# Gate reads in four buffers, differential heads asked for earlier, and two norms left unpinned, in a two-layer encoder kernel

## The chip, the cores and the metric

The kernel runs on one core of a Trainium2 chip. The metric is the device time of one execution in microseconds (us), given as the median of several runs. The engines are named as in the profile: PE is TensorE (matmuls and transposes), DVE is VectorE, ACT is ScalarE, POOL is GpSimd, and SP is the engine from whose queue all DMAs of this kernel are issued.

## The reference

Two layers of a bidirectional encoder over 512 tokens of width 1024, all in float32. Each layer computes one combined projection, three kinds of attention, a gated merge and an MLP:

```python
h = _rmsnorm(x, g_mix_pre[l])
z = h @ w_in[l]
...
o_a = _mla(c_q, c_kv, k_r, positions, ...)      # branch 0, 8 heads
o_b = _dilated(dq, dk, dv, rel_bias)            # branch 1
o_c = _diff(fq, fk, fv, positions, rel_bias, ...)  # branch 2, 4 heads, an RMSNorm for each head
gates = jax.nn.sigmoid(gz).reshape(b, s, N_BRANCH, D_MODEL)
merged = (gates[:, :, 0] * (o_a @ w_branch[l, 0])
          + gates[:, :, 1] * (o_b @ w_branch[l, 1])
          + gates[:, :, 2] * (o_c @ w_branch[l, 2]))
x = x + _rmsnorm(merged @ w_out[l], g_mix_post[l])
f = jnp.square(jax.nn.relu(_rmsnorm(x, g_mlp_pre[l]) @ w_up[l])) @ w_down[l]
x = x + _rmsnorm(f, g_mlp_post[l])
```

## The kernel before

**Products.** Every matrix is split into a high and a low part in float32r (names that end in hi and lo: `whi`, `wlo` for weights, `hhi`, `hlo` for the normed input, `moh`, `mol` for an MLA head's output, `ot` pairs for a branch's input). A product is three matmuls, hi·hi, hi·lo and lo·hi (`mm3`). ACT copies the high part, DVE (or POOL) subtracts it to get the low one.

**Order of the work.** The functions call engines in program order. A scheduling layer may reorder instructions on each engine by program order, buffers that come free and its own estimates. Where `in_order(True)` has been called, the wrapper `InOrder` pins ACT, DVE and SP instructions to program order. All DMAs go out through SP's one queue, in the order in which they stand there, so a DMA that waits for its data holds up those behind it. Each DMA also waits until the one eight places ahead of it has landed.

**The start.** x comes in four chunks of 128 tokens. `start(c)` norms a chunk (`norm_scale`: two squares on ACT, a short chain over DVE and POOL, and a scaling of 128x1024 on DVE, giving `xn`) and turns it (`norm_turn`: transposes `ntp` on PE, copies `hhi` on ACT, subtractions `hlo` on DVE). Chunks 0 and 1 are done first. `head_start` then runs the first half (tokens 0 to 255) of four blocks of the projection (`zq`), with `start(2)` behind the third and `start(3)` behind the fourth, and then the second halves. All of this is pinned. In the same stretch of time run `ld` and `lv`, small instructions of the set-up of the differential heads' lambda. A small table product (`pu`) follows on PE.

**The merge.** It runs over branches in the order 1, 2, 0, and in each over eight blocks of 128 output columns (`dp` = 0 to 3, two blocks each). A block is a gate read `gl` (256 KB from `gated` in DRAM), 12 matmuls `bp` into one of the two PSUM buffers of `mmt`, and a DVE operation that multiplies gate and product into `macc` (branch 1) or adds to it. A third block can't start on PE before the `macc` of the first has read its PSUM buffer. Branch 2's inputs are made here by `diff_norm`, once for each of four heads: two loads into `dn` (the head from `ond`, its norm factors from `rdr`), a multiplication on DVE, and an `ot` pair (copy on ACT, subtraction on DVE).

**What comes just ahead of the merge.** The last MLA head ends with matmuls `mo`, a copy `mot` (ACT), a product `ov` (DVE), the parts `moh` (ACT) and `mol` (DVE), and their two stores, which branch 0 reads back. `mot`, `moh` and `mol` live in the pool `tmp` of four buffers. The gates are computed ahead of it, in tiles `gt` with two buffers, and stored to `gated`. In the kernel before, `gl` shares these two buffers.

Of the kernel before, what the change touches and what calls it, by code (L numbers as in the profile page):

```python
# [9 lines left out]
F32 = mybir.dt.float32  # L10
# [56 lines left out]
class InOrder:  # L67


    def __init__(self, tc, eng):  # L70
        self.tc, self.eng, self.on = tc, eng, False

    def __getattr__(self, name):
        fn = getattr(self.eng, name)

        def call(*args, **kw):
            ins = fn(*args, **kw)  # L77
            if self.on:
                self.tc.keep_in_program_order(ins)
            return ins  # L80

        return call


def trunk(tc, a):
    nc = tc.nc
    with ExitStack() as ctx:
        _trunk(ctx, tc, nc, a)


def _trunk(ctx, tc, nc, a):
    sb = ctx.enter_context(tc.tile_pool(name="sb", bufs=1))
    ps = ctx.enter_context(tc.tile_pool(name="ps", bufs=1, space=PSUM))
    dr = ctx.enter_context(tc.tile_pool(name="dr", bufs=1, space=DRAM))
    act, vec, sync = InOrder(tc, nc.scalar), InOrder(tc, nc.vector), InOrder(tc, nc.sync)
    pool, pe = InOrder(tc, nc.gpsimd), nc.tensor

    def in_order(on, engines=(act, vec, sync)):
        for e in engines:
            e.on = on  # L100

    def mmt(name):
        return ps.tile([128, 512], F32, name=name, tag="mm", bufs=2)
# [7 lines left out]
    def pair(name, dt=F32R):  # L111

        t = sb.tile([128, 2, 512], dt, name=name, tag="pair", bufs=13)
        return t[:, 0], t[:, 1]

    def se(name, n, dt=F32):
        return sb.tile([128, n], dt, name=name, tag="se", bufs=6)
# [4 lines left out]
    def tmp(name, dt=F32):  # L122
        return sb.tile([128, 512], dt, name=name, tag="tmp", bufs=4)
# [4 lines left out]
    def f(x):  # L128
        return x.bitcast(F32)
# [4 lines left out]
    def mm3(out, wh, wl, xh, xl, first, last):  # L134
        mul(out, wh, xh, first, False)
        mul(out, wh, xl, False, False)
        mul(out, wl, xh, False, last)
# [50 lines left out]
    def split_w(raw, cols=1024, eng=None):  # L188
        hi = sb.tile([128, 1024], F32R, name="whi", tag="whi", bufs=4)
        lo = sb.tile([128, 1024], F32R, name="wlo", tag="wlo", bufs=4)  # L190
        act.activation(hi[:, :cols], raw[:, :cols], AF.Copy)
        (eng or vec).tensor_tensor(lo[:, :cols], raw[:, :cols], f(hi)[:, :cols], op=OP.subtract)
        return hi, lo

    def weights(src, cols=1024, eng=None):
        return split_w(load_w(src, cols), cols, eng)
# [18 lines left out]
    def norm_scale(x, g):  # L215

        st = small("nst", 2)
        xn = se("xn", D)
        for i in range(2):
            cs = slice(i * 512, (i + 1) * 512)  # L220
            act.activation(xn[:, cs], x[:, cs], AF.Square, accum_out=st[:, i:i + 1])
        vec.tensor_scalar(st[:, 0:1], st[:, 0:1], D * EPS, None, op0=OP.add)
        r = mean_rsqrt("n", st[:, 1:2], st[:, 0:1], D)
        vec.scalar_tensor_tensor(xn, x, r, g, op0=OP.mult, op1=OP.mult)
        return xn
# [156 lines left out]
    def by_chunk(t):  # L382

        return t.rearrange("p (j q) -> p q j", q=4)
# [39 lines left out]
    def chunked(t):  # L424
        return t.rearrange("p (c j) -> p c j", c=4)
# [45 lines left out]
    otd = {}  # L471
# [34 lines left out]
    def layer(l, h, first_w):  # L506
# [283 lines left out]
        for i in range(2):  # L790
            t = sb.tile([128, 512], F32R, name="wk", tag="ql", bufs=3)
# [131 lines left out]
        fill(1000)  # L923


        def diff_norm(hd, out):

            t = se("dn", 1024)
            o, rb = t[:, :512], t[:, 512:]
            sync.dma_start(o, ond[hd])  # L930
            sync.dma_start(rb, bass.AP(tensor=rdr.tensor, offset=rdr.offset + hd * 512, ap=[[0, 128], [1, 512]]))
            vec.tensor_tensor(chunked(o), chunked(o), by_chunk(rb), op=OP.mult)
            act.activation(out[0], o, AF.Copy)
            vec.tensor_tensor(out[1], o, f(out[0]), op=OP.subtract)

        macc = [None] * 8
        mh, ml = [None] * 8, [None] * 8
        for bi, b in enumerate((1, 2, 0)):
            ot = [pair("ot") for _ in range(4)]
            for kc in range(4):  # L940
                if b == 2:
                    diff_norm(kc, ot[kc])
                    continue
                for j in range(2):
                    sync.dma_start(f(ot[kc][j]), otd[b][kc, j])
            for dp in range(4):
                w = weights(wi("w_branch")[b * 4 + dp])
                hi = w[0].rearrange("p (d k n) -> p d k n", d=2, k=4)
                lo = w[1].rearrange("p (d k n) -> p d k n", d=2, k=4)
                for d2 in range(2):  # L950
                    d = dp * 2 + d2
                    t = sb.tile([128, 512], F32, name="gl", tag="gt", bufs=2)
                    sync.dma_start(t, gated[b, d])
                    p = mmt("bp")
                    for k4 in range(4):
                        mm3(p, hi[:, d2, k4], lo[:, d2, k4], ot[k4][0], ot[k4][1], k4 == 0, k4 == 3)
                    if bi == 0:
                        if d2 == 0:
                            mt = sb.tile([128, 2, 512], F32, name="macc", tag="pt", bufs=4)
                        macc[d] = mt[:, d2]  # L960
                        vec.scalar_tensor_tensor(macc[d], t, 1.0, p, op0=OP.add, op1=OP.mult)
                    else:
                        vec.scalar_tensor_tensor(t, t, 1.0, p, op0=OP.add, op1=OP.mult)
                        vec.tensor_tensor(macc[d], macc[d], t, op=OP.add)
                    if bi == 2:
                        mh[d], ml[d] = pair("mrg")
                        act.activation(mh[d], macc[d], AF.Copy, scale=0.5)
                        vec.scalar_tensor_tensor(ml[d], macc[d], 0.5, f(mh[d]), op0=OP.mult, op1=OP.subtract)


        gpost = load_g(wi("g_mix_post"), "gpost")
# [28 lines left out]
        def last_stage(blocks, lhs, xsrc, half_done, done, h_):  # L1000


            xns = {}
            turns = {c: (lambda c=c: norm_turn(xns[c], c, h_)) for c in range(4)}

            def one(acc, w, bi, c):
                hv, lv = (t.rearrange("p (k c) -> p k c", k=2) for t in w)
                for k2 in range(2):
                    k = bi * 2 + k2
                    lh, ll = (t[:, c * 128:(c + 1) * 128] for t in lhs[k])  # L1010
                    mul(acc, lh, hv[:, k2], k == 0, False)
                    mul(acc, lh, lv[:, k2], False, False)
                    mul(acc, ll, hv[:, k2], False, k == 7)

            for c0 in (0, 2):
                xos = {}
                for i in range(2):
                    xos[c0 + i] = se("xo", D)
                    sync.dma_start(xos[c0 + i], xsrc[c0 + i])
                accs = [pst("e0", "t") for _ in range(2)]  # L1020
                for bi in range(4):
                    w = weights(blocks(bi))
                    for i in range(2):
                        one(accs[i], w, bi, c0 + i)
                    if c0 and h_ is not None and bi % 2:
                        turns[bi // 2]()
                for i in range(2):
                    half_done(c0 + i, accs[i])
                accs = [pst("e1", "o") for _ in range(2)]
                ws = [weights(blocks(4 + bi)) for bi in range(4)]  # L1030
                for i in range(2):
                    for bi in range(4):
                        one(accs[i], ws[bi], bi, c0 + i)
                    xns[c0 + i] = done(c0 + i, accs[i], xos[c0 + i])
            return turns
# [5 lines left out]
        def half_out(c, p):  # L1041
# [3 lines left out]
        turns = last_stage(lambda i: wi("w_out")[i], lhs, xin, half_out,  # L1045
                           lambda c, p, xo: finish(ys[c][:, 0], p, ys[c][:, 1], sts[c], xo, c, gpost, xmid, gnext, h2),
                           h2)
# [136 lines left out]
        for qd in range(4):  # L1184
# [32 lines left out]
            last = l == DEPTH - 1  # L1217
# [18 lines left out]
            turns = last_stage(lambda i: wi("w_down")[i], ft, xmid, half_down, down, hn)  # L1236
# [3 lines left out]
    xs, xns, turns = [], {}, {}  # L1240

    def start(c):
        xns[c] = norm_scale(xs[c], g0)
        norm_turn(xns[c], c, h)
# [28 lines left out]
    ws = [split_w(raws[0], eng=pool)]  # L1273
    norm_turn(xns[1], 1, h)
    ws.append(split_w(raws[1]))
    for c in range(2, 4):
        turns[c] = lambda c=c: start(c)
    first = list(head_start(blocks, h, turns, "zq", ws))
    sync.dma_start(flip, a["flip"])
    in_order(False)  # L1280
    setup_bias()
    got = []
    def all_setup():
# [7 lines left out]
    for l in range(DEPTH):  # L1291
        nxt = layer(l, h, first)
        if l + 1 < DEPTH:
            h, turns = nxt
# [91 lines left out]
```

## Time and profile before

| | |
|---|---|
| median of 3 runs | 1870.62 us (1870.53 to 1878.24) |
| the profiled execution | 1869.85 us |
| its span, first to last instruction | 1868.1 us |
| PE busy | 1820.8 us, 97% of the span |
| DVE / ACT / POOL busy | 67% / 51% / 27% |
| mean granted TensorE clock | 0.998 |

The span is what the trace covers; the profiled execution is 1.75 us longer than it, and lies 0.77 us below the median. A granted clock of 1.00 in a stretch means that TensorE ran at the higher of its two levels throughout; 0.50 is the lower. Times of instructions are counted from the start of the span.

### The profile page before, as it was taken

To read this page: it belongs to the slowest core of one execution; us is meant where nothing else is said; L and a number is where in the kernel's file an instruction comes from. 1 tells how busy PE (TensorE), PEld (TensorE's weight loads), DVE (VectorE), ACT (ScalarE), POOL (GpSimd) and SP (SyncE) were. 2 spreads that over 40 slices of the span, in tenths; PEclk is the share of its full clock that TensorE was granted. 3 is DMA by queue.
4 is the path that set the end of the run, shared out by engine and by line. 5 is a ranking of instruction groups with operands and counts; after the bars stand their busy time and mean duration, and the time that the engine had idled before them with its cause. 6 is when DMAs were issued, how large, how long until landed. Compare 5 with 4: busy or idle time off the path is not lost.

```text
span 1868.1 us, 24762 instructions
## 1 busy us (share of the span) xinstructions
PE 1820.8 (97%) x9002; PEld 1523.6 (82%) x9002; DVE 1260.3 (67%) x2024; ACT 960.7 (51%) x1605; POOL 499.1 (27%) x367
## 2 busy tenths in 40 slices
PE   7999999999999999999999999999999999999998
PEld 6788788888777988788888887888887888878886
DVE  4855376656677786888674455675667779587965
ACT  4466355478525453443554554554783354543433
POOL 1344212331000242347123222114200015241542
PEclk9999999999999999999999999999999999999999
DMA  4365554346675432424453333544468562414243
GB/s 161 104 210 195 178 186 136 101 142 194 233 239 204 146 100 81 135 68 149 148 194 107 118 119 119 156 152 121 139 211 276 181 225 68 156 47 152 70 162 136
DMA packets 105843, 281.13 MB, mean 150 GB/s; under 512 B 13470, under 2 KB 19942, under 8 KB 105719
## 3 DMA queue, kind: packets, MB, share of 16 engines
q1 hardware_dynamic: 105718, 279.53, 46.0%
q8 instruction: 71, 1.16, 0.3%
q14 instruction: 54, 0.43, 0.1%
HBM read 228.50 MB, written 39.96 MB: 144 GB/s over the span
## 4 chain that ended last, share of the span: by engine, by line
PE 64%; DVE 10%; issue 4%; POOL 4%; DMA 3%; ACT 2%; SPq 0%; POOLq 0%; DVEq 0%; ACTq 0%
PE up L132 12%; PE gp L132 12%; PE p L132 9%; PE zq L132 7%; PE e L132 5%; PE bp L132 3%; DVE fr L77 3%; DVE wlo L77 3%; PE ms L132 2%; PE tp L465 2%; PE cp L132 2%; PE sd L132 2%; PE mo L132 1%; DVE fs L77 1%; POOL fr L77 1%
## 5 line engine op out<-in xcount | busy, mean ns | idle before, releaser
L77 ACT ACTIVATE whi<-wraw 128x1024 fp32r<-128x1024 f32 (+1 forms) x270 | 283.9, 1054 | 274.6 <-PE up L132 52.8
L77 DVE TENSOR_TENSOR wlo<-wraw,whi 128x1024 fp32r<-128x1024 f32 (+1 forms) x213 | 274.8, 1293 | 142.7 <-ACT whi L77 141.3
L77 POOL TENSOR_TENSOR wlo<-wraw,whi 128x1024 fp32r<-128x1024 f32 x57 | 139.3, 2447 | 369.5 <-ACT whi L77 369.5
L132 PE MATMUL up<-hlo,whi 128*128 128x512 f32 (+1 forms) x576 | 210.4, 366 | 0.0
L132 PE MATMUL up<-hhi,wlo 128*128 128x512 f32 (+1 forms) x576 | 210.4, 366 | 0.0
L132 PE MATMUL up<-hhi,whi 128*128 128x512 f32 (+1 forms) x576 | 209.9, 366 | 0.5 <-ACT hhi L77 0.5
L132 PE MATMUL p<-whi,fs 128*128 128x512 f32 x672 | 208.0, 389 | 0.0
L77 POOL TENSOR_TENSOR dw<-dw 128x1024 f32<-128x1024 f32 x48 | 132.1, 2755 | 144.6 <-DVE wlo L77 143.6
L132 PE MATMUL gp<-hhi,whi 128*128 128x512 f32 x384 | 153.0, 398 | 1.9 <-DVE ql L77 1.9
L132 PE MATMUL gp<-hhi,wlo 128*128 128x512 f32 x384 | 150.8, 393 | 0.3 <-POOL wlo L77 0.3
L132 PE MATMUL gp<-hlo,whi 128*128 128x512 f32 x384 | 150.3, 391 | 0.0
L132 PEld LDWEIGHTS p<-whi,fs 128*128 128x128 f32 x672 | 126.1, 188 | 26.1
L77 DVE TENSOR_TENSOR wlo<-dw,whi 128x1024 fp32r<-128x1024 f32 x84 | 138.0, 1662 | 13.7 <-POOL fr L77 10.9
L132 PE MATMUL zq<-hhi,whi 128*128 128x512 f32 (+1 forms) x384 | 138.7, 364 | 5.5 <-DVE ql L77 2.6
L132 PE MATMUL zq<-hhi,wlo 128*128 128x512 f32 (+1 forms) x384 | 138.7, 362 | 1.7 <-DVE wlo L77 1.0
L132 PE MATMUL zq<-hlo,whi 128*128 128x512 f32 (+1 forms) x384 | 138.3, 361 | 1.7 <-DVE hlo L77 1.7
L132 PE MATMUL p<-wlo,fs 128*128 128x512 f32 x336 | 131.5, 391 | 2.6 <-DVE wlo L77 2.6
L132 PE MATMUL bp<-ot,whi 128*128 128x512 f32 x384 | 120.3, 392 | 4.8 <-DVE macc L77 3.9
L77 ACT ACTIVATE whi<-dw 128x1024 fp32r<-128x1024 f32 x84 | 88.1, 1058 | 68.4 <-PE p L132 42.9
L132 PEld LDWEIGHTS up<-hlo,whi 128*128 128x128 f32 x576 | 108.6, 189 | 17.9 <-DVE hlo L77 0.4
L132 PEld LDWEIGHTS up<-hhi,whi 128*128 128x128 f32 x576 | 108.1, 188 | 18.4 <-ACT hhi L77 1.0
L132 PEld LDWEIGHTS up<-hhi,wlo 128*128 128x128 f32 x576 | 108.6, 189 | 17.5
(257 smaller groups left out, 4053.7 us busy)
## 6 DMA issues: line engine op xcount, KB each, us to landing
wraw<-in_w_up_dram SPq DMA_DIRECT2D x64, 512.0 KB, 4.3
wraw<-in_w_gate_dram SPq DMA_DIRECT2D x48, 512.0 KB, 3.7
dw<-in_w_down_dram SPq DMA_DIRECT2D x48, 512.0 KB, 3.4
btd<-ddram SPq DMA_DIRECT2D x64, 256.0 KB, 3.3
wraw<-in_w_out_dram SPq DMA_DIRECT2D x32, 512.0 KB, 3.4
wraw<-in_w_down_dram SPq DMA_DIRECT2D x32, 512.0 KB, 3.5
wraw<-in_w_dil_dram SPq DMA_DIRECT2D x24, 512.0 KB, 4.7
gated<-gt SPq DMA_DIRECT2D x48, 256.0 KB, 3.0
```

The lines of the kernel that those rows point to most:

```text
L77: ins = fn(*args, **kw)
L132: pe.matmul(out, lhsT, rhs, start=first, stop=last)
L465: pe.transpose(p[:, k * 128:(k + 1) * 128], e[:, k * 128:(k + 1) * 128], perm)
```

## The change

It has three parts.

1. The gate reads `gl` of the merge move from the two buffers that they share with the gate tiles to the pool `tmp` of four buffers, which the last MLA head's `mot`, `moh` and `mol` use too.
2. `diff_norm` becomes a generator. The eight loads of the four heads are called for in branch 1, behind the blocks of `dp` = 1; the arithmetic follows where branch 2 starts.
3. At the start, the pinning ends ahead of `head_start` instead of behind it. The norms of chunks 2 and 3 get a rule of their own: they are issued after the last pinned ACT and the last pinned DVE instruction.

```diff
@@ class InOrder
-        self.tc, self.eng, self.on = tc, eng, False
+        self.tc, self.eng, self.on, self.last = tc, eng, False, None
...
             if self.on:
                 self.tc.keep_in_program_order(ins)
+                self.last = ins.ins
@@ the merge
-        def diff_norm(hd, out):
+        def diff_norm(hd):
...
             sync.dma_start(rb, bass.AP(tensor=rdr.tensor, offset=rdr.offset + hd * 512, ap=[[0, 128], [1, 512]]))
+            yield
+            out = pair("ot")
             vec.tensor_tensor(chunked(o), chunked(o), by_chunk(rb), op=OP.mult)
             act.activation(out[0], o, AF.Copy)
             vec.tensor_tensor(out[1], o, f(out[0]), op=OP.subtract)
+            yield out
...
-            ot = [pair("ot") for _ in range(4)]
-            for kc in range(4):
-                if b == 2:
-                    diff_norm(kc, ot[kc])
-                    continue
-                for j in range(2):
-                    sync.dma_start(f(ot[kc][j]), otd[b][kc, j])
+            if b == 2:
+                ot = [next(n) for n in norms]
+            else:
+                ot = [pair("ot") for _ in range(4)]
+                for kc in range(4):
+                    for j in range(2):
+                        sync.dma_start(f(ot[kc][j]), otd[b][kc, j])
...
-                    t = sb.tile([128, 512], F32, name="gl", tag="gt", bufs=2)
+                    t = tmp("gl")
                     sync.dma_start(t, gated[b, d])
...
+                if b == 1 and dp == 1:
+                    norms = [diff_norm(kc) for kc in range(4)]
+                    for n in norms:
+                        next(n)
@@ the start
+    last = [act.last, vec.last]
+    in_order(False)
+
+    def later(c):
+
+        with tc.issue_after(last[0]), tc.issue_after(last[1]):
+            start(c)
+
     for c in range(2, 4):
-        turns[c] = lambda c=c: start(c)
+        turns[c] = lambda c=c: later(c)
     first = list(head_start(blocks, h, turns, "zq", ws))
     sync.dma_start(flip, a["flip"])
-    in_order(False)
```

How the instructions move, engine by engine, is seen in the order in which they stand. First ACT at the start, as one piece of the difference; `x_93` and `x_97` are chunks 2 and 3, the `whi` that moves is that of the fourth block.

```order
 L77 ACTIVATE whi<-wraw 128x1024 x2
 L77 ACTIVATE xn,nst<-x_93 128x512 x2
+L77 ACTIVATE whi<-wraw 128x1024
+L77 ACTIVATE xn,nst<-x_97 128x512 x2
 L77 ACTIVATE ld<-ld 128x1 x4
-L77 ACTIVATE hhi<-ntp 128x4x128 x2
-L77 ACTIVATE whi<-wraw 128x1024
-L77 ACTIVATE xn,nst<-x_97 128x512 x2
-L77 ACTIVATE hhi<-ntp 128x4x128 x2
+L77 ACTIVATE hhi<-ntp 128x4x128 x4
```

The fourth block's `whi` and the squares of chunk 3 stood behind the copies `hhi` of chunk 2, which wait for PE; now they stand ahead of them and of `ld`. On DVE the fourth block's `wlo` and the rest of chunk 3's norm move in the same way ahead of chunk 2's `hlo`. PE's order at the start stays as it was.

Next SP's queue where the merge of layer 0 begins, behind the last store of a gate; `gated_445` is the gates' tensor, `ond_1805` and `rdr_1804` hold the differential heads, `ot_0_446` the MLA output. Before:

```order
L77 DMA gl<-gated_445 128x512
L77 DMA dn<-ond_1805 128x512
L77 DMA dn<-rdr_1804 128x512
L77 DMA gl<-gated_445 128x512
L77 DMA dn<-ond_1805 128x512
L77 DMA gl<-gated_445 128x512
L77 DMA dn<-rdr_1804 128x512
```

After:

```order
L77 DMA dn<-ond_1805 128x512
L77 DMA dn<-rdr_1804 128x512
L77 DMA xo<-in_x_dram 128x1024
L77 DMA ot_0_446<-moh 128x512
L77 DMA ot_0_446<-mol 128x512
L77 DMA gl<-gated_445 128x512 x4
```

The first two rows of the second piece are the last of four such pairs: all eight loads of the heads come first, then a load of 512 KB for a later stage (`xo`), then the two stores of the last MLA head, and only then the first gate reads. Before, three gate reads stood ahead of these stores.

Last DVE in the same place. Before:

```order
L77 SCALAR_TENSOR_TENSOR macc<-gl,bp 128x512
L77 TENSOR_TENSOR ptl<-tp,pth 128x4x128
L77 TENSOR_TENSOR dn<-dn 128x512
L77 TENSOR_TENSOR ot<-dn,ot 128x512
L77 TENSOR_TENSOR ov<-mo,mot 64x256
L77 SCALAR_TENSOR_TENSOR macc<-gl,bp 128x512
L77 TENSOR_TENSOR wlo<-wraw,whi 128x1024
L77 TENSOR_TENSOR mol<-ov,moh 128x512
```

After:

```order
L77 TENSOR_TENSOR ptl<-tp,pth 128x4x128
L77 TENSOR_TENSOR dn<-dn 128x512 x2
L77 TENSOR_TENSOR ov<-mo,mot 64x256
L77 TENSOR_TENSOR ot<-dn,ot 128x512 x2
L77 TENSOR_TENSOR mol<-ov,moh 128x512
L77 TENSOR_TENSOR dn<-dn 128x512 x2
L77 TENSOR_TENSOR wlo<-wraw,whi 128x1024
L77 TENSOR_TENSOR ot<-dn,ot 128x512 x2
L77 SCALAR_TENSOR_TENSOR macc<-gl,bp 128x512 x4
```

The first `macc`, which frees the PSUM buffer for the third block, stood ahead of all this; now it stands behind the whole arithmetic of the four differential heads and a `wlo`. The second layer's merge moves in the same way.

## Rows read from the trace of the kernel before

**Rows 1.** Page, part 1: busy time of each engine.

```profile
PE 1820.8 (97%) x9002; PEld 1523.6 (82%) x9002; DVE 1260.3 (67%) x2024; ACT 960.7 (51%) x1605; POOL 499.1 (27%) x367
```

**Rows 2.** Waits of PE: waiter, releaser, us in total, times, longest.

```profile
PE tp L465 <- ACT sd L77: 5.1, 4, 1.9
PE bp L132 <- DVE macc L77: 3.9, 2, 3.0
...
PE bp L132 <- issue: 0.7, 1, 0.7
...
PE mo L132 <- DVE ptl L77: 0.5, 1, 0.5
```

**Rows 3.** Timeline of PE, start: start, us, operation, [idle before <-releaser].

```profile
27.71 0.28 PE L132 MATMUL zq<-hhi,wlo 128*128 128x256 f32 x1
27.83 1.03 PE L232 MATMUL ntp<-ident,xn 128*128 128x128 f32 x8
30.55 0.38 PE L132 MATMUL zq<-hhi,whi 128*128 128x256 f32 x1 [1.68 <-ACT whi L77]
...
31.81 0.38 PE L132 MATMUL zq<-hhi,wlo 128*128 128x256 f32 x1 [0.76 <-DVE nst L77]
...
35.95 1.13 PE L232 MATMUL ntp<-ident,xn 128*128 128x128 f32 x8
37.33 0.73 PE L132 MATMUL zq<-hhi,whi 128*128 128x256 f32 x4 [0.25 <-ACT hhi L77]
```

**Rows 4.** Timeline of ACT, same stretch.

```profile
28.47 1.08 ACT L77 ACTIVATE hhi<-ntp 128x512 fp32r<-128x512 f32 x2 [5.73 <-PE ntp L232]
29.44 1.06 ACT L77 ACTIVATE whi<-wraw 128x1024 fp32r<-128x1024 f32 x1
```

**Rows 5.** Windows at the start: busy (instructions) by engine, granted clock (PEclk), DMA share, GB/s.

```profile
32.60:36.10 3.50, 3.50 (x19) 3.50 (x18) 1.28 (x1) 0.00 (x0) 0.17 (x1) 0.52 0.17 32
...
56.50:60.00 3.50, 3.50 (x10) 2.53 (x9) 1.22 (x3) 1.45 (x2) 0.58 (x1) 0.52 0.20 40
```

**Rows 6.** Timeline of PE, layer 0's merge: the third block, and a later one.

```profile
494.35 0.62 PE L132 MATMUL bp<-ot,whi 128*128 128x512 f32 x2
...
508.56 0.73 PE L132 MATMUL bp<-ot,whi 128*128 128x512 f32 x2 [2.99 <-DVE macc L77]
```

**Rows 7.** Windows, the stretch behind that idle time (columns as in rows 5).

```profile
510.00:520.00 10.00, 10.00 (x45) 8.27 (x45) 4.32 (x7) 1.47 (x2) 0.00 (x0) 1.00 0.97 337
```

**Rows 8.** Timeline of SP's queue, same merge: when each DMA is issued.

```profile
487.12 0.39 SPq L77 DMA_DIRECT2D gl<-gated  x1
...
488.03 0.45 SPq L77 DMA_DIRECT2D dn<-rdr  x1
...
497.97 0.32 SPq L77 DMA_DIRECT2D ot<-mol  x1
498.34 1.60 SPq L77 DMA_DIRECT2D dn<-rdr  x1
```

**Rows 9.** Timeline of DVE, same merge.

```profile
495.07 0.42 DVE L77 TENSOR_TENSOR ov<-mo,mot 64x256 f32<-64x256 f32 x1
...
496.12 1.22 DVE L77 TENSOR_TENSOR wlo<-wraw,whi 128x1024 fp32r<-128x1024 f32 x1
497.26 0.68 DVE L77 TENSOR_TENSOR mol<-ov,moh 128x512 fp32r<-128x512 f32 x1
...
498.84 0.69 DVE L77 SCALAR_TENSOR_TENSOR macc<-gl,bp 128x512 f32<-128x512 f32 x1
...
505.11 1.06 DVE L77 TENSOR_TENSOR dn<-dn 128x512 f32<-128x512 f32 x1 [2.61 <-DMA dn<-rdr]
```

**Rows 10.** Tile `dn`: durations in ns min/median/max; us from issue to landing.

```profile
L77 DVE TENSOR_TENSOR ot<-dn,ot x8: 678/692/696, 494.3 to 1425.1; 128x512 fp32r<-128x512 f32 x8
...
DMA to landing us min/median/max: 4.6/5.2/6.7
```

**Rows 11.** Tile `gl`: us from issue to landing.

```profile
DMA to landing us min/median/max: 2.6/3.9/5.7
```

## Prediction

> **What bounds the kernel now.** I read the page's busy times first, then PE's waits, and then the timelines of the two places that the change touches. PE is busy for 1820.8 us of the span of 1868.1 [rows 1], so all idle time of PE is 47 us, and a change can win only from that, or lose by adding to it. The list of PE's waits shows how finely the idle time is scattered: the largest entry is 5.1 us in four pieces. The merges have 3.9 us in two waits for `macc`, 0.7 us that the trace puts down to issue, and 0.5 us in a wait of `mo` for `ptl` [rows 2]: 5.1 us in both layers. At the start PE stops for 1.68 us before the fourth block of `zq`, because `whi` comes late, for 0.76 us inside it, and for 0.25 us before the second halves [rows 3]. The timeline of ACT shows why: the pinned order has `hhi` of chunk 2 first, which waits for PE (ACT stood idle for 5.73 us before it), and the fourth block's `whi` starts only at 29.44 [rows 4]. The next thing to see is in the windows: in the 3.5 us behind this stop the granted clock is 0.52 in the mean, nearly all of it at the lower level [rows 5].
>
> **The start, part 3 of the change.** `whi`, `wlo` of the fourth block and the norm of chunk 3 move ahead of the copies that wait for PE. ACT was idle for 5.73 us there, so they cost nothing that PE would see: the `whi` takes 1.06 us [rows 4], the squares and `wlo` about as much each. The cover is that idle time; without it the start would stay as it is. PE then goes from the transposes of chunk 2, which end at 27.83 + 1.03 = 28.86, straight into the fourth block: 24 matmuls, at the distance of 0.12 us that the starts at 27.71 and 27.83 show, are 2.9 us, to 31.8. The transposes of chunk 3 (about 1.0 us) end at 32.8, and with the wait of 0.25 us kept, the second halves start at 33.1 instead of 37.33 [rows 3]: **4.2 us gained**. Of that, 2.4 us are idle time, 1.7 us the low clock ((1 - 0.52) x 3.5 us, [rows 5]). From below I bound it by the idle time alone, 2.4 us, if the low stretch only moves. From above I take 5.9 us, if the like stretch at 56.5 [rows 5], behind the small `pu` products, goes too; I see no reason for it, since these stay.
>
> **The merge, parts 1 and 2.** These must be costed together, since the order decides. Before, SP issued the first gate read at 487.12, and the store of `mol` only at 497.97 [rows 8]. Now eight loads of the heads, `xo` and the stores of `moh` and `mol` come ahead of all gate reads, and SP issues in order. So the first gate read can't start until DVE has made `mol`. DVE's first `macc` needs that read, and the third block on PE needs that `macc`. I follow the chain in layer 0.
>
> The loads of the heads start in the gate read's place, at 487.12, and one takes about 0.45 us to issue [rows 8]; the fourth, which completes the second head, goes out at 488.5 and lands 4.6 to 5.2 us later [rows 10], at about 493.4. On DVE follow the second `dn` (1.06 us), `ov` (0.42 us, [rows 9]) and two `ot` (0.69 us each, [rows 10]), so `mol` starts at about 496.3; before it was 497.26 [rows 9], with one `macc` and one `wlo` in place of the `ot`. From the start of `mol` to its store are 0.71 us (497.26 to 497.97), and SP's next DMA is 0.37 us behind that (497.97 to 498.34) [rows 8, 9]. The gate read is thus issued at 497.4 and, with the median of 3.9 us [rows 11], lands at 501.3.
>
> DVE's own queue says about the same. Behind `mol` (0.68 us) stand two `dn` (2.1 us), a `wlo` (1.2 us) and two `ot` (1.4 us) [rows 9, 10], which brings it from 496.3 to 501.7, or to 501.2 if starts follow each other a tenth closer than durations, as they do from `wlo` to `mol` (1.14 us apart for 1.22 us of work, [rows 9]). Two chains end together; to shorten one wouldn't help. With `macc` at 0.69 us [rows 9], PE's third block starts at about 502.1. Before, it started at 494.35 [rows 6] with no wait. **PE stalls for 7.7 us in each merge.** What is queued behind `macc` on DVE are only its three followers, and PE catches up at once. One stall and not more: the next gate reads are issued in one go, and the reads for the fifth block, issued when the first `macc` is done, have two blocks of 12 matmuls to land in (2.7 us each, by 45 matmuls in 10 us, [rows 7]).
>
> The bounds: with all DVE steps a tenth shorter and the landing at its shortest the stall is 6.7 us (DVE's chain then decides); with a gate read landing in 5.7 us [rows 11] it is 9.5 us.
>
> The waits of 5.1 us in both merges [rows 2] go, since the heads' arithmetic is finished by the stall, and the late load of the fourth head (DVE idle 2.61 us before it, [rows 9]) is early now. Net: 2 x 7.7 - 5.1 = **10.3 us lost**.
>
> **The clock behind the stalls.** At the start, 2.4 us of idle time were followed by 3.5 us at a mean of 0.52 [rows 5]. In the merge, 2.99 us of idle time [rows 6] were followed by ten at 1.00 [rows 7]. A stall of 7.7 us is over twice as long as either, and I take the row in which the level fell. I take a fall in each merge, at the price of the one seen: 1.7 us each, **3.4 us lost**. The bounds are nothing, and 3.4 us each, if the low level lasts twice as long as in either stretch of [rows 5].
>
> [...]
>
> **Sum.** -4.2 + 10.3 + 3.4 = +9.5 us on the profiled execution's 1869.85 us, 1879.4 us; the median of the runs lies 0.77 us higher, so the forecast is **1880.1 us**. A measurement of this kernel can tell about 0.5%, 9.4 us, from no change, so the forecast lies just on that bound, at 1880.0.
>
> **Rivals.**
> (a) The clock holds at the merges, as behind the wait of 2.99 us: +6.1 us, 1876.7 us. For it speaks [rows 7]; against it the start [rows 5] and the length of the stall. Chance 0.18.
> (b) The gate reads land late, since they meet the loads of `ot` and `xo`: 9.5 us of stall each, so -4.2 + (19.0 - 5.1) + 3.4 = +13.1 us, 1883.7 us. DMAs moved 337 GB/s with engines 97% busy a little later in the merge [rows 7], which makes it possible; but little else is asked for in the moment when the reads go out. Chance 0.13.
> (c) The start's gain is taken back: PE arrives earlier, but the waits of `tp` for `sd` on ACT, 5.1 us [rows 2], grow by as much. Then +13.7 us, 1884.3 us. Against it: ACT's work there hangs on PE's own results, which come earlier too. Chance 0.10.
> (d) The other side: the four buffers do what they allow, and the gate reads are in hand when the third block comes. Then no stall is added, the 5.1 us go, and with the start it is -9.3 us, 1861.3 us. It is decided by when the first gate read goes out: for a `macc` done by 494.35 it has to be issued before about 490. In SP's queue it stands behind the store of `mol`, which needs the last MLA head, and I see no way around that. Chance 0.05. [...]
>
> **Numbers.** The sum as forecast has 0.50, (a) 0.18, (b) 0.13, (c) 0.10, (d) 0.05; 0.04 is left for what I don't see. The range from 1874.0 to 1886.0 holds the forecast with its bounds (stalls of 6.7 to 9 us, a start between 2.4 and 5.9 us), (a), (b) and (c). Slower by over 0.5%: (b), (c) and half of the forecast's own chance, 0.47. Within 0.5%: (a), the other half, and what of (d) stays short of the bound, 0.49. Faster: 0.04, the rest of (d), whose -9.3 us lie on the bound, and a little for what I don't see.
>
> **What would show it.** In the profile after: the second halves of `zq` start near 33 us, with no wait for `whi` and a clock of 1.00 around 33 to 36; in each merge one wait of the third `bp` block for `macc` of 7 to 8 us, SP's first gate read right behind the store of `mol`, and a stretch of some 3.4 us at the low level behind the stall. No waits of `bp` for `macc` at the later place. The forecast is wrong if that one wait is under 5 us or the gate read is issued ahead of `mol`; if the clock stays at 1.00 behind the stall, it is (a).

## The result, and the profile after

The kernel after takes 1883.27 us (median of 9 runs, 1880.59 to 1883.81), the kernel before 1871.18 us (9 runs). The ratio is 1.006, with a 95% interval from 1.0051 to 1.0068: 11.2 us slower by the ratio (the medians lie 12.1 us apart), where +9.5 us was forecast. The profiled execution of after is the shortest of its nine, 1880.59 us with a span of 1878.5 us, 10.4 us over the span before.

The page's first part shows PE busy for only 0.6 us more than before [rows 1], so 9.8 of the 10.4 us are idle time:

```profile
PE 1821.4 (97%) x9002; PEld 1524.7 (81%) x9002; DVE 1260.7 (67%) x2024; ACT 961.2 (51%) x1605; POOL 498.9 (27%) x367
```

PE's list of waits says where. The columns are those of [rows 2]:

```profile
PE bp L133 <- DVE macc L77: 16.8, 2, 8.8
PE tp L466 <- ACT sd L77: 5.1, 4, 1.9
```

The wait for `macc` was 3.9 us and is 16.8 us, in two pieces, one for each merge. The wait for `sd` hasn't moved, so the start's gain was not taken back there.

**The start.** PE's timeline of after, answering [rows 3]:

```profile
28.23 1.03 PE L233 MATMUL ntp<-ident,xn 128*128 128x128 f32 x8
...
31.97 1.04 PE L233 MATMUL ntp<-ident,xn 128*128 128x128 f32 x8
33.26 0.74 PE L133 MATMUL zq<-hhi,whi 128*128 128x256 f32 x4 [0.25 <-ACT hhi L77]
```

The fourth block runs between the two rows of transposes with no wait, and the second halves begin at 33.26 instead of 37.33, 4.1 us earlier. PE came to the first row of transposes 0.4 us later than before in this execution (28.23, before 27.83 [rows 3]); counted from there the gain is 4.5 us. The window behind it is at the full clock, where [rows 5] had 0.52:

```profile
32.00:36.00 4.00, 3.75 (x31) 3.32 (x30) 1.29 (x2) 1.09 (x2) 0.00 (x0) 1.00 0.02 5
```

**The merge of layer 0.** First SP's queue, answering [rows 8]: all loads of the heads, `xo`, the store of `mol`, and then four gate reads.

```profile
483.24 0.38 SPq L77 DMA_DIRECT2D dn<-ond  x1
...
486.84 0.54 SPq L77 DMA_DIRECT2D dn<-rdr  x1
487.91 0.33 SPq L77 DMA_DIRECT2D xo<-in_x_dram  x1
...
493.87 0.32 SPq L77 DMA_DIRECT2D ot<-mol  x1
494.24 2.00 SPq L77 DMA_DIRECT2D gl<-gated  x4
```

DVE in the same stretch, answering [rows 9]:

```profile
489.14 1.09 DVE L77 TENSOR_TENSOR dn<-dn 128x512 f32<-128x512 f32 x1 [1.14 <-DMA dn<-rdr]
490.39 1.07 DVE L77 TENSOR_TENSOR dn<-dn 128x512 f32<-128x512 f32 x1 [0.16 <-DMA dn<-rdr]
...
493.16 0.69 DVE L77 TENSOR_TENSOR mol<-ov,moh 128x512 fp32r<-128x512 f32 x1
493.76 2.04 DVE L77 TENSOR_TENSOR dn<-dn 128x512 f32<-128x512 f32 x2
495.71 1.22 DVE L77 TENSOR_TENSOR wlo<-wraw,whi 128x1024 fp32r<-128x1024 f32 x1
496.85 1.29 DVE L77 TENSOR_TENSOR ot<-dn,ot 128x512 fp32r<-128x512 f32 x2
498.06 1.28 DVE L77 SCALAR_TENSOR_TENSOR macc<-gl,bp 128x512 f32<-128x512 f32 x2
```

The first `macc` follows `ot` with no idle time marked: DVE's own queue was the last thing it waited for. The gate read can't have been there long before: it was issued at 494.24, and the reads of this merge whose landing the trace has took 2.6 to 3.7 us. PE's side, layer 0 and then layer 1:

```profile
490.38 0.39 PE L133 MATMUL bp<-ot,wlo 128*128 128x512 f32 x1
498.79 1.22 PE L133 MATMUL bp<-ot,whi 128*128 128x512 f32 x2 [8.03 <-DVE macc L77]
...
1415.06 0.39 PE L133 MATMUL bp<-ot,wlo 128*128 128x512 f32 x1
1424.20 1.22 PE L133 MATMUL bp<-ot,whi 128*128 128x512 f32 x2 [8.75 <-DVE macc L77]
```

The pair of `bp` behind each stall takes 1.22 us where it took 0.62, or 0.73 behind the wait of 2.99 us [rows 6]: behind these two stalls the engine restarted at half rate. The windows behind them give the clock, 0.50 (column as in rows 5):

```profile
498.50:502.50 4.00, 3.71 (x9) 2.95 (x10) 0.83 (x2) 0.00 (x0) 0.00 (x0) 0.50 0.85 248
502.50:506.00 3.50, 3.50 (x16) 2.84 (x15) 0.69 (x1) 0.00 (x0) 0.00 (x0) 0.90 0.86 280
1424.00:1427.50 3.50, 3.30 (x8) 2.62 (x9) 0.74 (x2) 0.00 (x0) 0.00 (x0) 0.50 0.90 277
...
1427.50:1430.00 2.50, 2.50 (x11) 1.99 (x10) 0.69 (x1) 0.00 (x0) 0.00 (x0) 0.86 0.92 331
```

In layer 0 PE works at 0.50 from 498.79 to 502.5, and a mean of 0.90 over the next 3.5 us is another 0.7 us at 0.50: 4.4 us at half rate, 2.2 us lost. In layer 1, by the same count, 3.3 + 0.7 = 4.0 us, 2.0 us lost.

### The profile page after: what moved, and what is told of

Read it like the earlier page. It is cut to its first block, busy times and chain, and to the rows that moved or that the text cites. A ratio compares the mean times of both kernels' runs of the same rounds, so it can differ in the third digit from the quotient of the medians.

```text
span 1878.5 us, 24768 instructions
## 1 busy us (share of the span) xinstructions
PE 1821.4 (97%) x9002; PEld 1524.7 (81%) x9002; DVE 1260.7 (67%) x2024; ACT 961.2 (51%) x1605; POOL 498.9 (27%) x367
## 4 chain that ended last, share of the span: by engine, by line
PE 68%; DVE 9%; issue 4%; POOL 4%; ACT 2%; DMA 1%; SPq 0%; POOLq 0%; DVEq 0%; ACTq 0%
PE up L133 12%; PE gp L133 12%; PE p L133 9%; PE zq L133 7%; PE bp L133 7%; PE e L133 6%; DVE fr L77 3%; DVE wlo L77 2%; PE tp L466 2%; PE ms L133 2%; PE cp L133 2%; PE mo L133 2%; PE sd L133 2%; DVE fs L77 1%; POOL fr L77 1%
## 5 line engine op out<-in xcount | busy, mean ns | idle before, releaser
L133 PE MATMUL bp<-ot,whi 128*128 128x512 f32 x384 | 122.5, 399 | 16.8 <-DVE macc L77 16.8
```

What stands on the lines that cost most here:

```text
L133: pe.matmul(out, lhsT, rhs, start=first, stop=last)
```

## The experiments

Theory: `gl` in the pool of the last MLA head's tiles puts the gate reads behind that head's stores in SP's queue and the `macc` behind the heads' arithmetic on DVE; either one makes PE wait, and the wait costs a stretch at the low clock besides. Rivals: that the heads' early loads (part 2) do it; that only one of the two queues matters; that the clock costs nothing; that the start's gain goes again.

Ratios are to the kernel before, run beside it on the same chip, with 95% intervals.

**e1 and its repeat: the start alone.** The kernel before with part 3 of the diff.

> The kernel before with part 3 alone (the unpinned norms), gate reads and differential heads as before. If the start gives 4.1 us and all of it is kept, as the trace after shows up to the first merge (second halves of zq at 33.26 instead of 37.33), this is 4.1 us below before (ratio about 0.998), with the merges as in rows 6 and the waits of bp for macc at 3.9 us again. Rival, the gain is taken back later by a wait that grows: within 1 us of before.

Measured 0.9972 (0.9962 to 0.9982), 5.2 us faster. PE's waits for `macc` in it:

```profile
PE bp L133 <- DVE macc L77: 1.9, 2, 1.1
```

That was more than the 4.1 us of the start. In the profiled execution the second halves began at 32.44, 4.9 us earlier than before, and the waits for `macc` were 2 us shorter as well. So I ran it again.

> The kernel of e1 once more, beside e8 on one chip. It measured 0.9972 (0.9962 to 0.9982) of before, 6.0 us, where the start's trace shows 4.1 us. If the surplus is the scatter of runs, it comes out between 0.997 and 0.999 here.

Measured 0.9976 (0.9967 to 0.9985), 4.5 us faster. The 4.1 us lie inside both intervals. The start's gain is real and kept to the end, and this kernel beats both others. The second halves begin at 33.78 in this trace, 3.6 us earlier than before, and the waits for `macc` come to 1.8 us again; whether these are shorter because of the start isn't shown.

The two profiled executions of this one kernel differ at a place that no edit touches. Behind the `pu` products the clock fell in the first and not in the second (columns as in rows 5):

```profile
52.00:56.00 4.00, 4.00 (x11) 3.15 (x12) 2.10 (x4) 2.24 (x3) 0.57 (x1) 0.57 0.39 92
52.00:56.00 4.00, 4.00 (x16) 2.46 (x15) 2.28 (x4) 1.73 (x3) 0.58 (x1) 1.00 0.12 32
```

**e2: the gate reads alone.** The kernel before with one line changed:

```diff
-                    t = sb.tile([128, 512], F32, name="gl", tag="gt", bufs=2)
+                    t = tmp("gl")
```

> The kernel before with part 1 alone (gate reads in the four buffers), differential heads asked for as before, start pinned. If the move of the gate reads alone makes both stalls, the merges look as after: two waits of bp for macc of 8 to 9 us, first gate read behind the store of mol, and the time is that after plus the 4.1 us of the start, about 1886 us (ratio 1.008). Rival, the early request of the heads' loads (part 2) is what puts them ahead of the gate reads: then the stalls are gone here and the time is that of before.

Measured 1.0086 (1.0071 to 1.0102), 16 us slower, as expected. PE's waits:

```profile
PE bp L132 <- DVE macc L77: 17.2, 2, 8.6
```

This one line makes both stalls. Part 2 makes nothing: listed engine by engine, the order of the kernel with part 2 alone is row for row that of the kernel before, and the order with parts 1 and 2 is that of e2, so neither was run. The loads are called for in another place of the program and don't go out any earlier for it.

**e3: work for PE in the stall.**

```diff
+                    if bi == 0 and d == 1:
+                        pf = pst("fil", "s")
+                        for i in range(28):
+                            mul(pf, ot[i % 4][0][:, :128], ot[i % 4][0], True, True)
```

> The kernel after, with 28 matmuls of 128x512 put into PE's queue behind the second block of branch 1, whose product nobody reads (about 6.4 us of work inside each stall of 8 to 9 us). The stall in time stays, only PE isn't idle in it. If the lower clock behind the stalls costs time (4.0 to 4.4 us of PE work at half rate in each), the granted clock stays at 1.00 there and the time falls by 4 us or a little more against after, and the runs spread less. Rival, the low clock is hidden since DVE and the gate reads set the pace behind the stall anyway: the clock stays up and the time stays within 1 us of after.

Measured 1.0036 (1.0023 to 1.0048), against 1.006 (1.0051 to 1.0068) for the kernel after: 0.0024, 4.5 us, is what 28 useless matmuls in each layer gave back, by the two intervals between 1.7 and 7.3 us. PE's timeline of layer 0 shows the stall itself in place, 490.07 to 498.64, filled for 6.5 us:

```profile
490.07 6.51 PE L133 MATMUL fil<-ot 128*128 128x512 f32 x28
498.64 0.73 PE L133 MATMUL bp<-ot,whi 128*128 128x512 f32 x2 [2.07 <-DVE macc L77]
```

The windows behind it are at 0.86 in layer 0 and at 1.00 in layer 1:

```profile
500.00:510.00 10.00, 10.00 (x40) 8.14 (x39) 3.28 (x4) 1.06 (x1) 0.00 (x0) 0.86 0.77 257
...
1425.00:1435.00 10.00, 10.00 (x46) 8.29 (x45) 4.66 (x6) 2.12 (x2) 0.00 (x0) 1.00 0.93 306
```

So the low clock was a cost of its own. One short low stretch is left in layer 0, behind 2.07 us of idle time: the clock is 0.57 from 499 to 503, 1.7 us lost. By the clock, then, 4.2 - 1.7 = 2.5 us came back in this execution; whether the other 2 us of the 4.5 are more than scatter isn't shown.

**e5: gates early, heads first on DVE.** The kernel after, with the gate reads back in the two buffers and the first two `macc` issued behind the last `ot` of the heads; the heads are asked for behind the second block.

```diff
...
+                        if d == 1:
+                            heads = [list(diff_norm(kc))[-1] for kc in range(4)]
+                            for e, te, pm in ((0, t0, p0), (1, t, p)):
+                                with tc.issue_after(lastdve[0]):
+                                    vec.scalar_tensor_tensor(macc[e], te, 1.0, pm, op0=OP.add, op1=OP.mult)
...
```

> Gate reads early again (in the two buffers of the gate tiles, two of them issued ahead of most of the heads' loads), but DVE is made to do all arithmetic of the four differential heads ahead of the first macc, as after; start as after. If DVE's queue alone is enough for the stall, as the prediction says of the two chains, PE still waits for macc for 7 to 8 us in each merge, with the gate in hand long before, and the time is within 2 us of after. Rival, the late gate read is what holds macc: then DVE gets to the macc in time, and the stall is under 4 us.

Measured 1.0061 (1.0045 to 1.0078), the time of after. The gate read went out at 484.45, ahead of all the heads' loads, and the `macc` still came at 500.18. SP's and DVE's timelines:

```profile
484.45 0.38 SPq L77 DMA_DIRECT2D gl<-gated  x1
```

```profile
498.80 1.47 DVE L77 TENSOR_TENSOR ot<-dn,ot 128x512 fp32r<-128x512 f32 x2
500.18 1.28 DVE L77 SCALAR_TENSOR_TENSOR macc<-gl,bp 128x512 f32<-128x512 f32 x2
```

PE waited 17.8 us for `macc` in the two merges. DVE's queue alone is enough.

**e6: gates late, heads last on DVE.** The kernel after, with the heads' arithmetic behind the fourth `macc` (`mi` holds the `macc` instructions):

```diff
-                ot = [next(n) for n in norms]
+                with tc.issue_after(mi[3]):
+                    ot = [next(n) for n in norms]
```

> The kernel after (gate reads in the four buffers, behind the store of mol), but DVE does the differential heads' arithmetic only behind the first four macc. If the gate read alone is enough for the stall, PE still waits; but the heads' arithmetic also stood ahead of mol, so mol comes about 2.5 us earlier, the gate read goes out at about 491.5, lands at 495.5 and the stall is 5 to 6 us in each merge instead of 8 to 9; the time is 4 to 7 us below after. By the prediction's own sentence, that to shorten one chain wouldn't help, it would be the time of after. Rival, DVE's queue is the whole cause: no stall over 2 us.

Measured 1.0038 (1.0026 to 1.0051), 0.0022 or 4 us below after. The first gate read goes out at 492.19 instead of 494.24, since `mol` no longer stands behind the heads. PE's stalls:

```profile
496.74 1.22 PE L133 MATMUL bp<-ot,whi 128*128 128x512 f32 x2 [5.59 <-DVE macc L77]
...
1419.97 1.22 PE L133 MATMUL bp<-ot,whi 128*128 128x512 f32 x2 [5.67 <-DVE macc L77]
```

And on DVE the `macc` now has nothing ahead of it and waits for the read:

```profile
496.00 1.34 DVE L77 SCALAR_TENSOR_TENSOR macc<-gl,bp 128x512 f32<-128x512 f32 x2 [2.72 <-DMA gl<-gated]
```

The late gate read alone is enough too, for 5.6 us.

**e7: two buffers for branch 1, four for the rest.**

```diff
-                    t = tmp("gl")
+                    t = sb.tile([128, 512], F32, name="gl", tag="gt", bufs=2) if bi == 0 else tmp("gl")
```

> Parts 2 and 3, with branch 1's gate reads in the two buffers of the gate tiles and those of branches 2 and 0 in the four of tmp. SP issues the first gate reads as before, and later ones up to six at a time. If only the first reads of branch 1 matter, this is the time of the start alone, about 1867 us, or 1 us less, since few waits for gates are left later (0.2 us of PE). Rival, reads that go out early in fours and sixes push back the loads of weights and ot behind them in SP's queue: PE waits for wlo at branch 2 or 0, and it is slower than the start alone.

Measured 0.997 (0.9959 to 0.9982), the time of the start alone. Only branch 1's reads cost anything, and four buffers for the others win nothing that can be measured.

**e4: the heads' loads really early.** Gate reads in two buffers, and the loads called for behind dp = 0:

```diff
-                if b == 1 and dp == 1:
+                if b == 1 and dp == 0:
```

> Parts 2 and 3, with the gate reads left in the two buffers of the gate tiles, and the differential heads' loads asked for behind the blocks of dp = 0 instead of dp = 1. SP then issues two gate reads among the heads' loads, and all eight loads of the heads ahead of the store of moh, so that the fourth head no longer lands late. If the first macc sets the merge and the late head the one wait that was left, no third-block stall comes, the wait of 2.99 us of layer 0 shrinks too, and the time is 4.1 us (start) plus 2 to 4 us below before, 1863 to 1865 us (ratio 0.996 to 0.997). Rival, the early loads hold up the gate reads of the next blocks: no better than the start alone, 1867 us, or worse.

Measured 0.9984 (0.9975 to 0.9993), 3 us faster than before, and not the 6 to 8 us expected: the rival was nearer. The loads did go out early, the last at 488.53, and the fourth head landed in time. But then DVE took its work in earlier too:

```profile
495.95 2.04 DVE L77 TENSOR_TENSOR dn<-dn 128x512 f32<-128x512 f32 x2
497.91 0.68 DVE L77 SCALAR_TENSOR_TENSOR macc<-gl,bp 128x512 f32<-128x512 f32 x1
```

```profile
498.65 1.22 PE L133 MATMUL bp<-ot,whi 128*128 128x512 f32 x2 [2.67 <-DVE macc L77]
...
1417.49 0.72 PE L133 MATMUL bp<-ot,whi 128*128 128x512 f32 x2 [2.28 <-DVE macc L77]
```

PE's waits for `macc` come to 4.9 us, where e1, with the same start, has 1.9: in place of the wait of 2.99 us of before [rows 6] there is one at an earlier block.

**e8: the same, with the heads' arithmetic behind the third `macc`** (`issue_after(mi[2])`, as in e6).

> The kernel of e4 (gate reads in two buffers, heads' loads asked for behind dp = 0, start unpinned) with the heads' arithmetic put behind the third macc on DVE. In e4 PE waited 2.7 and 2.3 us for a macc that stood behind three dn on DVE. If DVE's order made these waits, they fall under 0.5 us each and the time is 2 us or more below the start alone (e1), about 1862 us (ratio 0.996 or less). Rival, the waits of 1 us that e1 still has come from elsewhere and a late head now holds up a later macc instead: the same time as e1, 0.997.

Measured 1.0001 (0.9992 to 1.001): a miss, slower than the start alone. The `macc` that was to come earlier now waits for its own gate, since SP's order changed with it and the third read went out at 493.61, behind `mol` and the last load of the heads. SP's row and DVE's:

```profile
493.61 1.60 SPq L77 DMA_DIRECT2D gl<-gated  x2
```

```profile
498.65 0.69 DVE L77 SCALAR_TENSOR_TENSOR macc<-gl,bp 128x512 f32<-128x512 f32 x1 [4.70 <-DMA gl<-gated]
```

The best version found is the start alone (e1) or with e7's line; the two can't be told apart.

## Why the prediction was right

The time, 1883.3 us, lies in the range from 1874 to 1886, 3 us above the forecast; the sign was right, and the case was the likeliest one. By its chances a time within 0.5% of before (0.49) was as likely as one slower by more (0.47), so that it came out at 0.6% and not under 0.5% is not to the forecast's credit.

**The start.** Forecast -4.2 us, measured -4.1 us to the second halves in the trace (-4.5 from the transposes on), -5.2 and -4.5 us in two comparisons of whole runs. The clock didn't fall behind it: from 28 to 37 it is 0.81 in the two profiles with the pinned start (before and e2) and 1.00 in all nine without. The like stretch behind `pu` stayed here (0.58 from 52 to 56), as forecast, but it isn't sure to, as e1's repeat shows. Right in each step.

**The stalls.** Forecast 7.7 us each, measured 8.03 and 8.75. The gate read followed `mol` by the 0.37 us that were read from before. Layer 1 is longer because its second head landed later, as DVE's rows there show:

```profile
1415.81 1.06 DVE L77 TENSOR_TENSOR dn<-dn 128x512 f32<-128x512 f32 x1 [1.25 <-DMA dn<-rdr]
...
1423.47 1.27 DVE L77 SCALAR_TENSOR_TENSOR macc<-gl,bp 128x512 f32<-128x512 f32 x2
```

From this `dn` to the first `macc` it takes 7.66 us here and 7.67 in layer 0 (490.39 to 498.06).

The term that was mis-sized is that landing: the forecast took 4.9 us from the issue of the second head's last load, and from issue to `dn` it was 5.7 us in layer 0 (484.66 to 490.39) and 6.5 in layer 1 (1409.34 to 1415.81). The gate's landing was over-sized: the forecast took 3.9 us, and layer 1's first read landed in 2.7, over 1 us ahead of its `macc`, so that there DVE's queue alone decided. That there is one stall and not more in each merge held.

**"To shorten one wouldn't help".** This step failed in part. To shorten the gate's chain doesn't help (e5, 17.8 us of waits). To shorten DVE's does: e6 has 5.6 us instead of 8 to 9, for the heads' arithmetic stands ahead of `mol` as well, so it was in both chains. I had costed them as two when they share their first part.

**Parts 1 and 2 together.** I costed them as one since the order showed them as one. All of it belongs to part 1 (e2); part 2, alone or beside part 1, changes no instruction's place.

**The clock.** Forecast a fall behind each stall, 3.4 us for both; the windows give 2.2 + 2.0 = 4.2 us. PE worked at half rate for 4.4 and 4.0 us, at the start for 3.4; the forecast's price was that of the shorter stretch. That e3 got 4.5 us back agrees only within its interval, since one of its low stretches was left. The trace has 0.50 behind the stalls of 8.03 and 8.75 us. In before, around the stretch of [rows 5], it reads 1.00 from 28.0 to 32.5, 0.50 from 33.0 to 36.0 and 1.00 from 36.5 to 38.0, with 0.72 and 0.87 in the two windows of 0.5 us between, in which it changed; 1.00 and 0.50 are the higher and the lower level of the forecast.

**The sum.** -4.1 + 16.8 - 5.1 + 4.2 = +11.8 us, against 10.4 us in the spans. Half of the 1.4 us between them is in the two lists of waits: PE's waits of `e` for `st` (0.8 us) and of `bp` for `gl` (0.2) are gone, one of `zq` for `vf` is 0.4 us shorter, and those of `e` for `wlo` are 0.7 longer. The rest I haven't followed. The stalls and the clock cost 2.2 us more than forecast; that the spans show only 0.9 us more (10.4 for 9.5) is owed to gains that the forecast didn't have, and so to luck. The other runs of after are up to 3.2 us longer than the profiled one, which no trace here explains.

**The rivals.** (a), the clock holds, is out by the windows. (b), late landings, isn't needed: the first read of after was there by 498.06, 3.8 us behind its issue, and not 5.7. (c) is out, since the wait for `sd` is 5.1 us as before and e1 kept its gain. (d) would have needed the gate read ahead of `mol`; e7, which has it there, is 5.6 us faster than before, not 9.3: of the 5.1 us of waits that were to go it still has 2.6 us for `macc` and 0.4 for `ptl`. In before the longest of them follows the late head [rows 9], not a gate.

## What to carry to other kernels

More buffers can cost more than they win if they come from a pool whose present tenants finish late: here the first load into them went behind the tenant's last use, and in SP's one queue behind all that the tenant's store waited for (the first gate read of layer 0 at 494.24 instead of 487.12); the move alone cost 16 us (e2). Look, in the order of the instructions, for what stands ahead of the first instruction that frees the matmul's accumulator, on the DMA queue and on the vector engine apart, and for work that is in both chains. Here the stalls of PE cost their length, 16.8 us, and the half-rate stretches behind them, 4.2 us, a fourth more.

## What the hardware showed that I had not expected

In these runs idle time of PE of under 3 us was followed by a lower clock at some places and not at others. Behind 2.99 us the clock stayed at 1.00 [rows 6, 7]; behind 2.67 us in e4's layer 0 the pair of `bp` took 1.22 us, as behind the stalls at 0.50, and the window from 500 to 510 had a mean of 0.92; behind 2.28 us in its layer 1 the pair took 0.72. Behind 2.07 us in e3's layer 0, which followed a stretch of steady matmuls, the window from 500 to 510 had a mean of 0.86. And behind `pu` one and the same kernel had 0.57 in one execution and 1.00 in another (e1 and its repeat). So in these runs the length of the idle time alone doesn't tell whether the level falls.
